# Soft mixture of experts, first 512 rows of x: from a casting load to float32 loads on two hardware queues with a cast on chip, and the first expert's products in two halves

## The chip, the cores and the metric

The kernel runs on one core of one Trainium2 chip. The metric is the device time of one execution in microseconds (us); lower is better. The profile is one execution taken by the hardware profiler; its times count from the start of its span. Engines: PE (TensorE, matmuls; PEld is its weight load), DVE (VectorE), ACT (ScalarE), POOL (GpSimd), SP (SyncE). A "q" behind an engine's name means its sequencer, which also issues transfers.

## The reference

```python
def setup_inputs():
    batch, seq, hidden, n_experts, expert_hidden = 16, 512, 512, 8, 2048
    ...

def reference(x, router_logits, expert_weights):
    probs = softmax(router_logits, axis=-1)
    ...
    for e in range(n_experts):
        expert_out = np.matmul(x, expert_weights[e])
        output += probs[:, :, e:e+1] * expert_out
    return output.astype(np.float32)
```

(The softmax is written out in the reference, with the maximum taken off first.) There are 8192 rows of x with 512 columns, 8 experts with weights of 512 x 2048 each, and an output of 8192 x 2048 float32. Every row's output is the sum over all experts of its probability times its product with that expert's weights.

## The kernel before, in words

**Arithmetic.** A row's sum over experts is one long product: x scaled by the probabilities of the experts, laid side by side, times the experts' weights stacked. The kernel cuts this product into quarters (rows in pairs of 256-row blocks, output columns in halves of 1024, experts in halves of four) and applies a seven-product scheme on two levels in place of eight products, with sums and differences of blocks made on DVE. So most of the program is: DVE makes a scaled left operand (`z`, float16), PE multiplies it with a block of weights (`w`, float16) into PSUM (`ps`), ACT or DVE evicts the result, and transfers carry it to HBM. These stages are laid out by a planner written by hand (`stages`, `at`, `slack`), which issues DVE's tasks by their costs; they begin at line 334 and the diff does not touch them.

**The opening, lines 80 to 332.** This is where the change lies. It computes a first product for 512 rows (row tiles `j` = 0 to 3 of 128 rows each, two from each of two 256-row blocks of x that lie 512 rows apart), four experts `e` and 1024 output columns (two blocks `n` of 512), without the two-level scheme, while the first weights are still on their way:

- Lines 80 to 89: ACT loads its table (L82), DVE clears a tile, and PE runs `WARM` = 10 matmuls on zeros (L89), which compute nothing that is used.
- `load_lg0(0)` (L206): the 512 rows' logits on SP's queue. `cast_x(0)`, `cast_x(2)` (L207, L208): two transfers on POOL's queue, of 256 rows of x each, float32 in HBM, cast by the transfer to float16 in `xs0`. [...]
- L213 to L219: the weights of the first block (`b11`), cast by POOL's queue too. `behind()` holds them behind what was issued so far. The first expert's load, for `n` = 0, is in two parts of two chunks (`c` = 0, 1 and 2, 3), the others are whole. Then two more x transfers (`cast_x(4)`, `cast_x(6)`) for later rows, and the last weights.
- `early_p(0)` (L244): the softmax of the 512 rows, on DVE with one ACT exponential (L179). `diag_e(e)` (L246): for expert e, DVE makes four diagonal matrices of its probabilities, 0.64 to 0.68 us each.
- `early_z0(e, d)` (L249): for each row tile j, four matmuls of 128 columns that transpose the four 128-column chunks of x and scale its rows at once (x's chunk times the diagonal matrix), into one PSUM bank; DVE (even j) or ACT (odd j) evicts the bank to `z0[j][:, e]` as float16.
- `load_logits()` (L279): SP loads the rest of the logits. Two memsets on DVE (L280, L281) keep these loads from being issued before DVE has come this far.
- The loop at L308: for `n` and `e`, 16 matmuls of 512 columns (4 chunks x 4 row tiles), chunk outermost, into four banks `ps[j]`. In the first round of `n`, `early_z0(e + 2)` stands ahead of the products of experts 0 and 1. So PE's order before is: transposes of experts 0, 1, 2; products of expert 0; transposes of expert 3; products of experts 1, 2, 3; then the second block.

**What sets the order.** Each engine runs its own list in order. `dve()`, `act()`, `sp()`, `pool()` and `mm()` record each instruction; those from `dve` and `act` stay in program order on their engine, so ACT's evictions and casts come in the order in which the code names them. Transfers of one queue are issued in order by their engine; a transfer that waits holds those behind it in the same list. PSUM has eight banks, given out by `bank()`.

Of the kernel before, what the change touches and what calls it, by code (L numbers as in the profile page):

```python
# [31 lines left out]
def kernel(  # L32
# [7 lines left out]
    nc = tc.nc  # L40
    P = 128
    f16 = mybir.dt.float16
    f32 = mybir.dt.float32
# [3 lines left out]
    B, S, H = x.shape  # L47
    E, _, EH = expert_weights.shape
    T = B * S
    C = H // P  # L50
    HE = E // 2
    NB = 512
    NH = EH // 2
    WARM = 10
    HQ = 256
    NHQ = T // HQ
    NI = NHQ // 2
# [2 lines left out]
    x_f = x.flatten_outer_dims()  # L60
# [3 lines left out]
    wpool = ctx.enter_context(tc.tile_pool(name="wpool", bufs=15))  # L64
# [9 lines left out]
    def h_tile(shape, dtype):  # L74
        return hpool.tile(shape, dtype, name="h", tag="h")

    def half():
        return h_tile([P, NB], f32)

    tiny = cpool.tile([P, 1], f32, name="tiny")  # L80
    nc.vector.memset(tiny, 0.0)
    nc.scalar.activation(out=tiny, in_=tiny, func=mybir.ActivationFunctionType.Exp)  # L82

    with tc.tile_pool(name="psum0", bufs=1, space=bass.MemoryType.PSUM) as psum0:
        zero = h_tile([P, NB], f16)
        nc.vector.memset(zero, 0.0)
        every = psum0.tile([P, 8, NB], f32, name="every")
        for i in range(WARM):
            nc.tensor.matmul(every[:, i % 8, :], zero[:, 0:P], zero, start=True, stop=True)  # L89
# [5 lines left out]
    def note(i):  # L95
        last[i.ins.engine] = i.ins
        if ordered[0]:
            tc.keep_in_program_order(i)

    def dve(i):  # L100
        last[i.ins.engine] = i.ins
        tc.keep_in_program_order(i)

    act = dve
# [12 lines left out]
    def sp(o, i):  # L117
        note(nc.sync.dma_start(out=o, in_=i))

    def pool(o, i, **how):  # L120
        note(nc.gpsimd.dma_start(out=o, in_=i, **how))  # L121

    def bank():
        return psum.tile([P, NB], f32, name="ps", tag="ps")

    def mm(ps, z, w, start, stop):
        note(nc.tensor.matmul(ps, z, w, start=start, stop=stop, skip_group_check=True))  # L127
# [3 lines left out]
    def new_w():  # L131
        return wpool.tile([P, K8, NB], f16, name="w", tag="w")
# [31 lines left out]
    def inner_sums(b, t7=None):  # L164

        w = {1: b[0, 0], 2: b[1, 0], 3: b[1, 1], 7: t7 or b[0, 1]}

        def step(p, x, y):
            if p not in w:
                w[p] = new_w()  # L170
            tt(w[p], x, y, SUB)
        return w, {5: lambda: step(5, b[0, 1], b[0, 0]), 6: lambda: step(6, b[1, 1], w[5]),
                   4: lambda: step(4, b[1, 0], w[6]), 7: lambda: step(7, b[1, 1], b[0, 1])}
# [15 lines left out]

    xs0 = new_w()  # L190

    ROWS = ("(p j) h -> p j h", "(j p) h -> p j h")

    def cast_x(j):
        pool(xs0[:, ds(j, 2), :], x_f[ds(j * HQ, HQ), :].rearrange(ROWS[j // 4], p=P))

    def load_lg0(t):
        rows = lg_f.rearrange("(q h) e -> q h e", h=2 * HQ)[ds(2 * t, 2), 0:HQ]
        tile_ = lg0[t].rearrange("p (q j) e -> p q j e", j=2)
        if t == 0:  # L200
            sp(tile_, rows.rearrange("q (p j) e -> p q j e", p=P))
        else:
            for q in range(2):
                sp(tile_[:, q], rows[q].rearrange("(j p) e -> p j e", p=P))
    lg0 = [cpool.tile([P, 4, E], f32, name=f"lg0_{t}") for t in range(2)]
    load_lg0(0)  # L206
    cast_x(0)  # L207
    cast_x(2)  # L208
    ident = cpool.tile([P, P], f16, name="ident")
    nc.vector.memset(ident, 1.0)  # L210
    nc.gpsimd.affine_select(out=ident, in_=ident, compare_op=mybir.AluOpType.is_equal, fill=0.0, base=0,
                            pattern=[[-1, P]], channel_multiplier=1)
    b11 = {kn: new_w() for kn in BLOCKS}  # L213
    with behind():
        for kn in BLOCKS[:3]:
            cast_block(11, kn, b11[kn], 2 if kn == (0, 0) else 1)
    cast_x(4)
    cast_x(6)
    cast_block(11, BLOCKS[3], b11[BLOCKS[3]])  # L219

    def early_p(t):
        if t == 0:
            return softmax(lg0[t], 4, cpool.tile([P, HE, 4], f16, name="ph0"))
        pf = softmax(lg0[t], 4, cpool.tile([P, HE, 4], f32, name="pf0"))
        odd = pf.rearrange("p e (q j) -> p e q j", j=2)[:, :, :, 1]
        tt(odd[:, 0:2], odd[:, 0:2], odd[:, 2:4], ADD)
        ph = cpool.tile([P, HE, 4], f16, name="ph1")
        dve(nc.vector.tensor_copy(ph, pf))
        return ph

    def diag(p):

        d = h_tile([P, 4, P], f16)
        tt(d, ident.unsqueeze(1).to_broadcast([P, 4, P]), p.to_broadcast([P, 4, P]), MUL)
        return d

    def evacuate(o, ps, i):
        if i % 2:
            act(nc.scalar.copy(o, ps))
        else:  # L240
            dve(nc.vector.tensor_copy(o, ps))  # L241

    z0 = [zpool.tile([P, HE, C, P], f16, name="z", tag="z") for j in range(4)]
    ph0 = [early_p(0)]  # L244

    def diag_e(e):  # L246
        return diag(ph0[0][:, e].unsqueeze(2))

    def early_z0(e, d):  # L249
        for j in range(4):  # L250
            ps = bank()
            for c in range(C):
                mm(ps[:, ds(c * P, P)], xs0[:, j, ds(c * P, P)], d[:, j], c == 0, c == C - 1)
            evacuate(z0[j][:, e], ps.rearrange("p (c t) -> p c t", c=C), j)
# [5 lines left out]
    def diag_j(j):  # L260
        return diag(ph0[1][:, :, ds(j % 4, 1)])

    def early_xp1(j, d):
        t, rows = j // 2 - 2, ds(j % 2 * P, P)
        ps = bank()
        for c in range(C):
            mm(ps[:, ds(c * P, P)], xs0[:, j, ds(c * P, P)], ident, c == 0, c == C - 1)
        evacuate(xp1[t][0][:, :, rows], ps.rearrange("p (c t) -> p c t", c=C), 0)
        ps = bank()
        mm(ps, ones, d.rearrange("p e t -> p (e t)"), True, True)  # L270
        evacuate(xp1[t][1][:, :, rows], ps.rearrange("p (e t) -> p e t", e=HE), 1)
# [7 lines left out]
    def load_logits():  # L279
        dve(nc.vector.memset(lg_all[:, 0, 0:1], 0.0))  # L280
        dve(nc.vector.memset(lg0[1][:, 0, 0:1], 0.0))  # L281
        load_lg0(1)
        for r in range(R):
            sp(lg_all[ds(r * NHQ, NHQ)], lg_v[r])

    def softmax_of_all():

        pf = softmax(lg_all, J, h_tile([P, E, J], f32))
        pq = h_tile([P, HE, J], f32)
        tt(pq, pf[:, 0:HE], pf[:, HE:E], ADD)  # L290
        low = ds(P // 2, P // 2)
        pv = pf.rearrange("p (s e) j -> p s e j", s=2)[low]
        tt(pv[:, :, 0:2], pv[:, :, 0:2], pv[:, :, 2:4], ADD)
        tt(pq[low, 0:2], pq[low, 0:2], pq[low, 2:4], ADD)
        ph = h_tile([P, 3 * HE, J], f16)
        act(nc.scalar.copy(ph[:, 0:E], pf))
        act(nc.scalar.copy(ph[:, E:], pq))
        for r in range(R):
            sp(p_dram[:, :, ds(r * J, J)], ph[ds(r * NHQ, NHQ)])

    kept = [dram.tile([2, HQ, NB], f32, name=f"kept_{i}") for i in range(NI)]

    ds_ = [diag_e(0), diag_e(1)]
    early_z0(0, ds_[0])
    ds_.append(diag_e(2))
    load_logits()
    early_z0(1, ds_[1])
    for n in range(2):  # L308
        ps = [bank() for _ in range(4)]
        for e in range(HE):  # L310
            if n == 0 and e < 2:
                early_z0(e + 2, ds_[e + 2])
                if e == 0:
                    ds_.append(diag_e(3))
            if n == 0 and e == 2:
                ph0.append(early_p(1))
                ds_ = [diag_j(j) for j in range(4, 8)]
                softmax_of_all()
                w, sums = inner_sums(b11, new_w())
            for c in range(C):  # L320
                for j in range(4):
                    mm(ps[j], z0[j][:, e, c], b11[e // 2, n][:, e % 2 * C + c, :],
                       e + c == 0, e == HE - 1 and c == C - 1)
            if n == 1:
                for j in ((4, 5), (6, 7), (), ())[e]:
                    early_xp1(j, ds_[j - 4])
                if e == 1:
                    sums[5]()
        for j in range(4):
            o = half()  # L330
            act(nc.scalar.copy(o, ps[j]))
            sp(kept[j // 2][n].rearrange("(p j) m -> j p m", j=2)[j % 2], o)
# [706 lines left out]
```

## Time and profile before

| | us |
|---|---|
| three runs, median (lowest to highest) | 1377.73 (1377.30 to 1377.74) |
| the profiled execution | 1377.86 |
| its span, first to last instruction | 1376.2 |
| PE busy | 1368.5 (99% of the span, 6390 matmuls) |
| DVE busy | 1108.8 (81%) |
| POOL busy | 412.3 (30%) |
| ACT busy | 183.3 (13%) |
| HBM read, written | 207.65 MB, 156.43 MB: 265 GB/s over the span |

The steady part of the kernel is matmuls of 512 columns, recorded with a mean of 379 ns each; they are pipelined, and start 0.216 us apart (16 in 3.46 us). A time "to landing" of a transfer counts from the start of its issue to the completion that others can wait for. Where a row of the timeline says `[0.80 <-DMA w<-in_x_dram]`, the engine was idle for 0.80 us before it, and the last thing that released it was that transfer. A row "x16" merges 16 instructions that follow each other, and its time runs from the first one's start to the last one's end; as matmuls overlap, the next row can start before that.

### The profile page before, as it was taken

The page shows a single profiled execution, that of the slowest core. Times are in us where ns is not written, and L with a number is a line of the kernel's source. Part 1 is how long each engine was busy: PE and PEld are TensorE (multiplying, and loading weights), DVE is VectorE, ACT ScalarE, POOL GpSimd, SP SyncE. Part 2 cuts the span into 40 slices and gives each one's busy share as a digit, 9 for nine tenths or more (in the row PEclk, how much of TensorE's full clock was granted, in tenths as well). Part 3 has the DMA queues.
Part 4 walks back from the last instruction along what each step waited for, and adds up shares of the span by engine and source line. Part 5 has one row for each costly group of instructions (what it writes and reads, how often), then busy time and mean ns, then how long its engine had stood idle before and what let it go on. Part 6 is the DMA issues. An engine that isn't in the chain of part 4 may idle for free.

```text
span 1376.2 us, 17481 instructions
## 1 busy us (share of the span) xinstructions
PE 1368.5 (99%) x6390; PEld 622.3 (45%) x6390; DVE 1108.8 (81%) x1290; ACT 183.3 (13%) x317; POOL 412.3 (30%) x652
## 2 busy tenths in 40 slices
PE   9999999999999999999999999999999999999998
PEld 4444444444444444444444444444444444444444
DVE  5846757679789888798887988889888898898782
ACT  3222111100011111111111100000000000222221
POOL 3222333231223342334332122333323322232321
PEclk9999999999999999999999999999999999999999
DMA  9997999999898998999897997988888979998785
GB/s 186 229 255 207 212 250 260 252 297 381 235 311 267 279 282 249 267 260 264 252 275 255 348 383 208 241 233 207 232 231 231 231 219 309 228 197 186 167 147 101
DMA packets 191271, 338.02 MB, mean 246 GB/s; under 512 B 52944, under 2 KB 86992, under 8 KB 187472
## 3 DMA queue, kind: packets, MB, share of 16 engines
q0 software_dynamic: 88688, 185.12, 55.8%
q1 hardware_dynamic: 98464, 123.34, 31.1%
q10 hardware_dynamic: 4032, 28.44, 5.3%
q8 instruction: 50, 0.82, 0.2%
q14 instruction: 37, 0.30, 0.1%
HBM read 207.65 MB, written 156.43 MB: 265 GB/s over the span
## 4 chain that ended last, share of the span: by engine, by line
PE 91%; issue 4%; DMA 3%; POOL 1%; DVE 1%; POOLq 0%; ACT 0%; DVEq 0%
PE ps L127 91%; POOL out_dram L121 1%; DMA out_dram<-h 1%; DMA w<-wd 1%; DMA w<-in_x_dram 0%; DVE h L107 0%; DVE z L107 0%; DVE u L107 0%; POOL wd L121 0%; DVE z L241 0%; POOL w L121 0%; ACT h L991 0%; POOLq L121 0%; DVEq L107 0%; DVE lg L281 0%
## 5 line engine op out<-in xcount | busy, mean ns | idle before, releaser
L127 PE MATMUL ps<-w,z 128*128 128x512 f16 x5416 | 1177.5, 379 | 2.1 <-DVE h L107 1.7
L127 PEld LDWEIGHTS <-z 128*128 128x128 f16 x5416 | 529.7, 98 | 639.8 <-issue 2.6
L121 POOL DMA_DIRECT2D out_dram<-h x380 | 249.2, 675 | 742.5 <-ACT h L536 369.1
L107 DVE TENSOR_TENSOR h<-ps,h 128x512 f32<-128x512 f32 x415 | 282.6, 688 | 207.8 <-PE ps L127 190.1
L107 DVE TENSOR_TENSOR z<-xT,pT 128x2048 f16<-128x2048 f16 x220 | 267.2, 1218 | 12.1 <-DMA xT<-xs 8.3
L127 PE MATMUL ps<-w,d 128*128 128x512 f16 x880 | 199.1, 379 | 0.0
L127 PEld LDWEIGHTS <-d 128*128 128x128 f16 x880 | 86.1, 98 | 103.8
L107 DVE TENSOR_TENSOR z<-z,d 128x2048 f16<-128x2048 f16 x110 | 132.2, 1217 | 0.0
L107 DVE TENSOR_TENSOR w<-w 128x1024 f16<-128x1024 f16 (+2 forms) x92 | 101.0, 1103 | 6.3 <-DMA wd<-w 3.9
L525 ACT COPY h<-ps 128x512 f32<-128x512 f32 x90 | 52.9, 587 | 375.0 <-PE ps L127 314.0
L536 ACT COPY h<-ps 128x512 f32<-128x512 f32 x64 | 37.6, 587 | 486.1 <-PE ps L127 459.7
L107 DVE TENSOR_TENSOR d<-z 128x1024 f16<-128x1024 f16 x110 | 75.4, 686 | 6.8 <-PE ps L127 5.0
L107 DVE TENSOR_TENSOR z<-z,u 128x2048 f16<-128x2048 f16 x64 | 78.4, 1225 | 2.2
L107 DVE TENSOR_TENSOR u<-xT,pT 128x2048 f16<-128x2048 f16 x64 | 78.0, 1219 | 0.0
L522 ACT COPY h<-ps 128x512 f32<-128x512 f32 x90 | 52.8, 587 | 173.8 <-PE ps L127 160.2
L121 POOL DMA_DIRECT2D wd<-w x86 | 48.4, 586 | 36.9 <-DVE w L107 27.4
L121 POOL DMA_DIRECT2D w<-in_expert_weights_dram x65 | 48.9, 783 | 34.2 <-DMA wd<-w 24.1
L107 DVE TENSOR_TENSOR ps<-ps,h 128x512 f32<-128x512 f32 (+1 forms) x66 | 45.4, 689 | 12.9 <-PE ps L127 12.9
L121 POOL DMA_DIRECT2D kept<-h x56 | 30.9, 551 | 75.5 <-ACT h L525 46.9
L107 DVE TENSOR_TENSOR h<-h 128x512 f32<-128x512 f32 (+2 forms) x69 | 45.1, 675 | 0.2
L518 ACT COPY ps<-ps 128x512 f32<-128x512 f32 x45 | 25.7, 572 | 114.6 <-PE ps L127 114.6
L107 DVE TENSOR_TENSOR z<-z 128x2048 f16<-128x2048 f16 x32 | 39.2, 1225 | 1.1
(47 smaller groups left out, 98.1 us busy)
## 6 DMA issues: line engine op xcount, KB each, us to landing
out_dram<-h POOLq DMA_DIRECT2D x380, 256.0 KB, 6.2
pT<-p_dram SPq DMA_DIRECT2D x140, 256.0 KB, 6.1
w<-wd ACTq DMA_DIRECT2D x27, 1024.0 KB, 9.8
h<-kept SPq DMA_DIRECT2D x100, 256.0 KB, 5.8
xT<-x SPq DMA_DIRECT2D x87, 256.0 KB, 5.8
wd<-w POOLq DMA_DIRECT2D x72, 256.0 KB, 5.8
w<-in_expert_weights_dram POOLq DMA_DIRECT2D x35, 512.0 KB, 10.1
h<-out_dram SPq DMA_DIRECT2D x68, 256.0 KB, 5.5
```

The costliest lines, as they stand in the source:

```text
L107: dve(nc.vector.tensor_tensor(out=o, in0=a, in1=b, op=op))
L121: note(nc.gpsimd.dma_start(out=o, in_=i, **how))
L127: note(nc.tensor.matmul(ps, z, w, start=start, stop=stop, skip_group_check=True))
L518: act(nc.scalar.copy(self.banks["b"], x))
L522: act(nc.scalar.copy(o[tn], q if p == 5 else x))
L525: act(nc.scalar.copy(o[TN[p]], b if p == 2 else x))
L536: act(nc.scalar.copy(o[tn], b))
```

## The change

1. The first 512 rows of x no longer come as float16 through POOL's casting queue. Two plain float32 transfers into a new tile `x32` take their place: rows of the first block on ACT's queue, as the first thing in the program, rows of the second on SP's queue behind the first logits. `x32` takes a buffer of the weight pool.
2. Four casts on chip fill `xs0`: tiles 0, 1 and 3 on ACT, tile 2 on DVE. ACT's list there becomes: cast tile 0, cast tile 1, evict tile 1, cast tile 3, further evictions. DVE's: diagonals of expert 0, evict tile 0, cast tile 2, evict tile 2, diagonals of experts 1 and 2, the two memsets, further evictions.
3. The products of expert 0 for the first block come in two halves of the rows: all chunks for tiles 0 and 1, then the transposes of expert 1, all chunks for tiles 2 and 3, then the transposes of expert 2. The transposes of expert 3 follow the products of expert 1. All other products stay as they were.
4. `WARM` is 9 and not 10.

```diff
-    WARM = 10
+    WARM = 9
...
+    x32 = wpool.tile([P, 4, H], f32, name="x32", tag="w")
+    x_first = [x_f[ds(2 * q * HQ, HQ), :].rearrange("(p j) h -> p j h", p=P) for q in range(2)]
+    nc.scalar.dma_start(out=x32[:, 0:2, :], in_=x_first[0])
     tiny = cpool.tile([P, 1], f32, name="tiny")
...
     load_lg0(0)
-    cast_x(0)
-    cast_x(2)
+    sp(x32[:, 2:4, :], x_first[1])
...
-    def early_z0(e, d):
-        for j in range(4):
+    def early_z0(e, d, js=range(4)):
+        for j in js:
...
-    ds_ = [diag_e(0), diag_e(1)]
-    early_z0(0, ds_[0])
-    ds_.append(diag_e(2))
+    ORDERS = ([(c, j) for c in range(C) for j in range(4)],
+              [(c, j) for h in range(2) for c in range(C) for j in (2 * h, 2 * h + 1)])
+    ds_ = [diag_e(0)]
+    for j in range(2):
+        act(nc.scalar.copy(xs0[:, j, :], x32[:, j, :]))
+    early_z0(0, ds_[0], (0, 1))
+    dve(nc.vector.tensor_copy(xs0[:, 2, :], x32[:, 2, :]))
+    act(nc.scalar.copy(xs0[:, 3, :], x32[:, 3, :]))
+    early_z0(0, ds_[0], (2, 3))
+    ds_ += [diag_e(1), diag_e(2)]
     load_logits()
-    early_z0(1, ds_[1])
     for n in range(2):
         ps = [bank() for _ in range(4)]
         for e in range(HE):
-            if n == 0 and e < 2:
-                early_z0(e + 2, ds_[e + 2])
-                if e == 0:
-                    ds_.append(diag_e(3))
+            if n == 0 and e == 1:
+                ds_.append(diag_e(3))
...
-            for c in range(C):
-                for j in range(4):
-                    mm(ps[j], z0[j][:, e, c], b11[e // 2, n][:, e % 2 * C + c, :],
-                       e + c == 0, e == HE - 1 and c == C - 1)
+            for c, j in ORDERS[n == 0 and e == 0]:
+                mm(ps[j], z0[j][:, e, c], b11[e // 2, n][:, e % 2 * C + c, :],
+                   e + c == 0, e == HE - 1 and c == C - 1)
+                if n == 0 and c == C - 1 and (e, j) in ((0, 1), (0, 3), (1, 3)):
+                    early_z0(1 + e + j // 3, ds_[1 + e + j // 3])
```

In the lists of instructions that the two programs give each engine, this is all that differs; behind the opening, every engine's list is the same in both.

More of the change, by code (lines that the diff above doesn't have):

```diff
@@ L190 @@
     xs0 = new_w()
-    ROWS = ("(p j) h -> p j h", "(j p) h -> p j h")
     def cast_x(j):
-        pool(xs0[:, ds(j, 2), :], x_f[ds(j * HQ, HQ), :].rearrange(ROWS[j // 4], p=P))
+        pool(xs0[:, ds(j, 2), :], x_f[ds(j * HQ, HQ), :].rearrange("(j p) h -> p j h", p=P))
     def load_lg0(t):
```

## The prediction

> **What bounds the kernel now.** I read the busy table first: PE is busy 1368.5 of 1376.2 us. Then the chain of waits, to see whether anything ahead of the steady matmul stream sets the end. Its first 40 us:
>
> ```profile
> 1.33 0.67 POOL w L121
> 2.00 4.86 DMA w<-in_x_dram
> 6.91 0.41 PE ps L127 x4
> 7.35 0.69 DVE z L241
> 8.04 0.60 DVE h L107
> 8.64 0.05 DVE lg L281
> 8.69 31.51 PE ps L127 x180
> ```
>
> The reader is to see that the end hangs on the x load (cast by the DMA, issued by POOL) until 6.9 us, on VectorE until 8.7, and from there on TensorE alone (in the chain over the whole span that piece of PE runs on from 8.69 for 776.79 us). So the opening can matter only through the moment at which TensorE begins to run without a gap. The waits by engine say the same: PE waits in five places, 4.0 us in all over the span.
>
> The opening in the timeline, engine by engine (start, length, engine, line, operation, count):
>
> ```profile
> 1.29 4.45 PE L89 MATMUL every<-h 128*128 128x512 f16 x10 [1.29 <-DVE h L86]
> 5.64 0.77 PEld L127 LDWEIGHTS <-w 128*128 128x128 f16 x8 [0.80 <-DMA w<-in_x_dram]
> 6.40 0.69 DVE L241 CAST z<-ps 128x512 f16<-128x512 f32 x1 [0.94 <-PE ps L127]
> 6.62 0.59 ACT L239 CAST z<-ps 128x512 f16<-128x512 f32 x1 [3.21 <-PE ps L127]
> 9.76 3.63 PE L127 MATMUL ps<-w,z 128*128 128x512 f16 x16
> 13.22 1.06 PE L127 MATMUL ps<-h,w 128*128 128x128 f16 x16
> 14.11 13.98 PE L127 MATMUL ps<-w,z 128*128 128x512 f16 x64
> 24.82 0.62 ACT L296 CAST h<-h 128x512 f16<-128x512 f32 x1 [3.37 <-DVE h L107]
> ```
>
> One expert's scaled transposes (early_z0, 16 matmuls of 128 columns) hold TensorE from 13.22 to 14.11, 0.89 us; one expert's products (16 of 512 columns) from 9.76 to 13.22, 3.46 us. Issue to landing of single transfers (KB written, last figure in us), the first x half issued at 1.33, the first two chunks of the first expert at 2.90, the logits at 0.81:
>
> ```profile
> w<-in_x_dram POOLq DMA_DIRECT2D x1, 256.0 KB, 4.3
> w<-in_expert_weights_dram POOLq DMA_DIRECT2D x1, 256.0 KB, 6.8
> lg<-in_router_logits_dram SPq DMA_DIRECT2D x1, 16.0 KB, 1.9
> ```
>
> So x's first half landed at 5.6, its second at 6.86 (the end of the DMA piece in the chain), and the first weights at 9.7: TensorE's weight load of 9.75 had waited 0.17 us for them.
>
> **The break-even.** The order of instructions of the two programs differs in the opening alone; afterwards every engine's list is the same. Before, products begin at 9.76 with three experts' transposes done. After, they begin with one done; two blocks of 0.89 follow among the products. If TensorE then runs without a gap, the change breaks even where the first product starts at 9.76 - 2 x 0.89 = 7.98 us. Call the new start P; the effect is P - 7.98.
>
> **The change, part by part.**
> *Removed from POOL:* two issues (0.67 and about 0.6 us, with first x at 1.33 and first weights at 2.90), so weights are issued 1.57 us sooner. *Added:* one x half each on ACT's and SP's queues. An issue costs ACT about 0.4 us (SP's logit issues take 0.42 to 0.46, and ACT's last store 0.37), which moves the table load of 0.81 to 1.28 us later; its exp of the logits at 3.18 has 0.88 us of idle time before it, so this is hidden, and would cost up to 0.4 if that cover went. On SP the x half goes behind the first logits and ahead of all other loads; the only one issued right behind it is half of the second logits, needed at 15.19. *One warm-up matmul less:* ten take 4.45 us, so the nine end about 0.43 sooner, at 5.1 for what follows them. Worth something only if x is ready then.
>
> *Landing of x's first half (L).* No row shows 512 KB in float32 on an idle hardware queue. Low end: 0.81 + 1.9 (logit row) + 1.27 (what the second half took after the first, 6.87 - 5.60, which is 512 KB read) = 4.0; the logits' own data is in the 1.9, so 3.8 is thinkable. High end: 0.81 + 4.3 (this very load, other queue) + 1.27 for the other half interleaved with it = 6.4. I take 4.6, the hardware row plus half of the second half's 1.27: its fixed part is from the nearest row in kind of queue, and the two queues share the engines. By the load's own row without sharing it would be 5.1.
>
> [...]
>
> *The new serial chain behind L.* ACT's list is now: cast row tile 0, cast tile 1, evict tile 1's transposes, cast tile 3. So: 0.05 to react (landing 5.60, weight load 5.64); two casts at 0.62 (the ACT cast of 128x512 float32 from SBUF, row L296), 1.24; tile 1's four matmuls until they can be evicted 0.76 (5.64 to 6.40 for four) plus 0.04; eviction 0.59; third cast 0.62; 0.04; four matmuls and on to the product, 0.16 for the load and 4 x 0.056 (0.89 / 16), 0.4. Sum 3.74, P = L + 3.7. VectorE's branch is shorter: tile 0's eviction 0.69 and tile 2's cast (no row; between 0.35, half of the nearest, and 0.69 of an eviction from PSUM) end before ACT's third cast. Break-even: L = 4.3. With 4.6, P = 8.3 and the effect is **+0.3 us**.
> *Floor.* However early x comes, TensorE is on its warm-up until 5.1; eight matmuls to eviction 0.82 (6.62 - 5.80), then 0.59 + 0.62 + 0.04 + 0.4: P at least 7.6. The gain cannot pass 0.4 us.
>
> *Weights.* The first chunks: at best 1.33 + 6.8 - 2 x 1.27 = 5.6 (both x loads gone from ahead), at worst 1.33 + 6.8 = 8.1 (the same bytes still ahead, through interleaving). Both lie before 8.3, so I cost this wait at nothing; behind an early x it would be next. The next chunks (needed at P + 0.87 = 9.2) come 1.3 later, 6.9 to 9.4. The expert's second load had 13.7 as its landing and is needed at P + 2 x 1.73 + 2 x 0.89 = 13.5, now issued 1.57 sooner.
> *Moved on VectorE:* two diagonals (2 x 0.65) and the two marker memsets that release the logit loads (8.59 before) now stand behind tile 2's eviction, about 1 us later. The logits feed reductions at 15.19 that end in diagonals by 19.5, which TensorE first reads at 28.15, and probabilities stored at 25.8 whose reloads SP issues only at 42.05, behind stores. That cover is 8 us and more; nothing.
> Casts and evictions add about 2.5 us of ACT and VectorE work there; both idle in that stretch.
>
> **Sum.** Span 1376.2 + 0.3; the profiled execution took 1377.86, of which 1.66 lie around the span, and stands 0.13 over the median of 1377.73. On the median: 1378.0 us.
>
> **Rivals.**
> 1. *x is early after all* (L of 3.8 to 4.0). For it: the logits' 1.9 us. Against it: they are 16 KB, and x on POOL's queue took 4.3. P = 7.6 to 7.7, effect -0.3 to -0.4: 1377.4.
> 2. *The loads interleave, the first expert's weights with them* (L of 5.5 to 6.4). For it: DMA's share is 0.8 to 1.4 in every half microsecond from 4.0 us on. P = 9.2 to 10.1, +1.2 to +2.1: about 1379.2. The logits could also be held behind x's packets: they would delay the first diagonal, which must then end 1.0 us later (4.8 now, 5.8) before it costs anything.
> 3. *TensorE stays slow* (slower than before). The records of its matmuls change in the opening: 128-column matmuls have a mean of 284 ns in 5.7 to 6.2 us and 220 from 6.9 on, and the warm-up's ten of 512 columns have 631 against 379 later; the step falls near 6.2, 4.9 us after the first of them, though the granted clock shows 1.00 all along. Ten warm-ups in 4.45 us are 0.43 apart, products 0.216: half the pace. After the change TensorE idles from 5.1 until 5.4, again between tiles 0 and 1, and for over a microsecond ahead of tile 2, where before there were gaps of 0.06, 0.33 and 0.27. If that makes it stay slow past P, every us of it costs 0.5. From 4.9 us of it (as long as the first stretch) with the 0.3 it is +2.75, 1380.5: from there it decides. One us or two, and it is 1379.
> [...]
> 4. *That it doesn't do what it says* is excluded by the lists of instructions: ACT's first entry is the x load.
>
> **How the numbers follow.** Forecast (between -0.2 and +0.9) 0.44; rival 1 0.18; rival 2 0.20; rival 3 0.18, about half of it at 4.9 us or more. The range of 1377.2 to 1379.7 reaches over rival 1 and most of rival 2, and leaves out the long form of rival 3 and the end of rival 2; the forecast's own is 1377.5 to 1378.6. 0.2% of 1377.7 is 2.76 us, about what a measurement of this kernel can tell from no change. Faster by that is beyond the floor of 0.4 us: 0.02, for what I overlooked. Slower by that needs the long form of rival 3, or rivals 2 and 3 together: 0.10. Within it: 0.88.
>
> **What would show it.** In the new timeline: x's first half casts on ACT at 4.65 (L); the products of 512 columns first at 8.3 (P) and no gap behind them; ACT's third cast ending 0.4 before P; weight loads waiting for no weights; the first products 0.216 apart, else rival 3; the first diagonal still ending at 4.8. Wrong altogether would be a gap of TensorE later than 20 us that was not there, or a span that moves by another amount than P - 7.98.

## The result, and the profile after

| | median, us | runs | lowest to highest |
|---|---|---|---|
| before | 1377.74 | 6 | 1377.30 to 1378.42 |
| changed | 1382.47 | 6 | 1381.36 to 1384.00 |

The ratio is 1.0035 with a 95% interval of 1.0022 to 1.0048: slower by 4.7 us, 3.0 to 6.6 by the interval. The profiled execution of the changed kernel took 1382.42 us, its span 1380.7 (1376.2 before). The prediction had 1378.0.

The opening after the change, from the timeline of TensorE (start, length, engine, line, operation, count):

```profile
1.29 4.02 PE L92 MATMUL every<-h 128*128 128x512 f16 x9 [1.29 <-DVE h L89]
7.05 1.01 PE L130 MATMUL ps<-h,w 128*128 128x128 f16 x8 [1.73 <-DVE h L110]
8.75 1.11 PE L130 MATMUL ps<-h,w 128*128 128x128 f16 x8 [0.69 <-DVE w L309]
9.66 3.62 PE L130 MATMUL ps<-w,z 128*128 128x512 f16 x8
13.07 1.35 PE L130 MATMUL ps<-h,w 128*128 128x128 f16 x16
14.26 1.89 PE L130 MATMUL ps<-w,z 128*128 128x512 f16 x8
```

Three things are in these rows. The first transposes begin at 7.05, after a wait of 1.73 us for VectorE's diagonal (h, L110), not for x. The first product begins at 9.66, against a break-even of 7.98. And the first eight products hold TensorE from 9.66 to 13.07, 3.41 us, where the second eight (14.26 to 15.99) need 1.73: the first eight run at half pace. The records of the granted clock in this trace begin with full pace at 13.68.

Why the diagonal is late stands in the chain of waits:

```profile
0.81 3.94 DMA lg<-in_router_logits_dram
4.78 0.20 DVE h L180
5.23 0.24 ACT lg L182
6.21 0.70 DVE h L110
7.05 0.60 PE ps L130 x4
```

The chain now begins with the logits, 16 KB that landed 1.9 us after issue before the change and 3.9 after it. They hold up x as well: its first half had landed at 4.57, but ACT's list has the exponential of the logits ahead of the two casts.

```profile
5.23 0.23 ACT L182 ACTIVATE lg<-lg 128x32 f32<-128x32 f32 x1 [2.46 <-DVE lg L110]
5.36 1.12 ACT L307 CAST w<-x 128x512 f16<-128x512 f32 x2
```

The transfers issued in the first microsecond (KB, then us to landing) show what is beside the logits:

```profile
x<-in_x_dram ACTq DMA_DIRECT2D x1, 512.0 KB, 3.8
lg<-in_router_logits_dram SPq DMA_DIRECT2D x1, 16.0 KB, 3.9
```

Both were issued at 0.81, on two queues, and the small one landed after the large one. In the packet records of the trace, x's half runs first (128 packets from 1.9 us on), 255 of the logits' 256 packets start only after 3.0, and the second x half (SP's queue) and the weights (POOL's) follow nearly one after the other, most of the one from 4.0 on and all of the other from 5.1 on.

A second loss lies at 31 us. VectorE, ACT and TensorE in the timeline after the change, and behind them the same reduction and the same evictions before it:

```profile
21.96 0.17 DVE L180 TENSOR_REDUCE h<-lg 128x4 f32<-128x32 f32 x1
27.57 0.63 ACT L182 ACTIVATE h<-h 128x512 f32<-128x512 f32 x1 [4.93 <-DVE h L110]
31.57 0.62 ACT L296 CAST h<-h 128x512 f16<-128x512 f32 x1 [3.37 <-DVE h L110]
32.40 2.04 ACT L336 COPY h<-ps 128x512 f32<-128x512 f32 x4
33.12 0.38 PE L130 MATMUL ps<-ident,w 128*128 128x128 f16 x4 [1.37 <-ACT h L336]
```

```profile
15.19 0.19 DVE L177 TENSOR_REDUCE h<-lg 128x4 f32<-128x32 f32 x1 [0.26 <-DMA lg<-in_router_logits_dram]
25.65 2.04 ACT L331 COPY h<-ps 128x512 f32<-128x512 f32 x4
```

The first reduction of the remaining logits starts at 21.96 (15.19 before), though the load that it needs was issued at 11.72 and had landed at 17.5 (5.8 us). VectorE's list has the evictions of expert 3's transposes ahead of it, and those transposes moved behind expert 1's products (20.34 and not 13.22). ACT's list has its evictions of the first block's banks (L336) behind the exponential and casts of that softmax, so they start at 32.40 (25.65 before), and TensorE, which needs a bank for the next transposes, stands idle.

From the starts of the same matmuls in both traces, the changed kernel is 3.66 us behind from 18 to 28 us, 5.26 behind from 34 on, and 4.27 at the last one: later waits of TensorE for VectorE have shrunk, most of it near 1180 us. These late waits differ from execution to execution: from 34 us to the end, the lag changes by -1.4 to +0.6 us in the traces of the runs below. The first figure splits: 1.68 of late first product (9.66 - 7.98), 1.68 of half pace in eight products (3.41 - 1.73), 0.29 in the transposes behind them (13.07 to 14.26 is 1.19, such a block is 0.89).

### The profile page after: what moved, and what is told of

Its sections match the earlier page's. It is cut to its first block, busy times and chain, and to the rows that moved or that the text cites. A ratio compares the mean times of both kernels' runs of the same rounds, so it can differ in the third digit from the quotient of the medians.

```text
span 1380.7 us, 17484 instructions
## 1 busy us (share of the span) xinstructions
PE 1370.4 (99%) x6389; PEld 623.2 (45%) x6389; DVE 1109.3 (80%) x1291; ACT 184.6 (13%) x320; POOL 411.1 (30%) x650
## 4 chain that ended last, share of the span: by engine, by line
PE 77%; issue 12%; DMA 6%; POOL 4%; DVE 1%; ACT 0%; SPq 0%; POOLq 0%; ACTq 0%; DVEq 0%
PE ps L130 77%; POOL out_dram L124 3%; DMA out_dram<-h 2%; DMA wd<-w 1%; DMA w<-wd 1%; POOL wd L124 1%; DVE h L110 1%; DMA xs<-in_x_dram 1%; DMA h<-kept 0%; DMA lg<-in_router_logits_dram 0%; POOL w L124 0%; SPq L402 0%; DVE z L110 0%; DVE u L110 0%; DVE z L241 0%
## 5 line engine op out<-in xcount | busy, mean ns | idle before, releaser
L110 DVE TENSOR_TENSOR h<-ps,h 128x512 f32<-128x512 f32 x415 | 282.4, 688 | 208.3 <-PE ps L130 188.3
L110 DVE TENSOR_TENSOR z<-xT,pT 128x2048 f16<-128x2048 f16 x220 | 267.1, 1218 | 12.0 <-DMA xT<-xs 6.9
L110 DVE TENSOR_TENSOR z<-z,d 128x2048 f16<-128x2048 f16 x110 | 132.2, 1217 | 0.0
L110 DVE TENSOR_TENSOR w<-w 128x1024 f16<-128x1024 f16 (+2 forms) x92 | 101.0, 1103 | 5.2 <-DMA wd<-w 2.9
L110 DVE TENSOR_TENSOR d<-z 128x1024 f16<-128x1024 f16 x110 | 75.4, 686 | 6.8 <-PE ps L130 5.0
L110 DVE TENSOR_TENSOR z<-z,u 128x2048 f16<-128x2048 f16 x64 | 78.4, 1225 | 2.2
L110 DVE TENSOR_TENSOR u<-xT,pT 128x2048 f16<-128x2048 f16 x64 | 78.0, 1218 | 0.0
L110 DVE TENSOR_TENSOR ps<-ps,h 128x512 f32<-128x512 f32 (+1 forms) x66 | 45.4, 689 | 12.6 <-PE ps L130 12.5
L110 DVE TENSOR_TENSOR h<-h 128x512 f32<-128x512 f32 (+2 forms) x69 | 45.1, 675 | 0.4 <-ACT h L530 0.3
L110 DVE TENSOR_TENSOR z<-z 128x2048 f16<-128x2048 f16 x32 | 39.2, 1225 | 1.1
```

The lines of the kernel that those rows point to most:

```text
L110: dve(nc.vector.tensor_tensor(out=o, in0=a, in1=b, op=op))
```

## The experiments

Each row is against the kernel before on the same chip (its median in brackets). The last column is read from the one traced execution of each run: how far the matmuls that the kernel before starts at 34 us start behind it.

| run | median, us | against before | 95% interval of the ratio | behind at 34 us, trace |
|---|---|---|---|---|
| changed kernel | 1382.47 (1377.74) | +4.7 | 1.0022 to 1.0048 | 5.3 |
| 16 warm-ups | 1380.09 (1377.57) | +2.5 | 1.0009 to 1.0028 | 3.1 |
| logits first, one queue | 1381.05 (1377.57) | +3.5 | 1.0019 to 1.0043 | 6.5 |
| expert 3's transposes back | 1381.17 (1377.57) | +3.6 | 1.0016 to 1.0035 | 3.1 |
| logits first, two queues | 1381.19 (1377.59) | +3.6 | 1.0017 to 1.0036 | 3.4 |
| warm-ups and transposes back | 1378.67 (1377.36) | +1.3 | 1.0002 to 1.0019 | 1.7 |
| all three repairs | 1378.79 (1377.59) | +1.2 | 0.9997 to 1.0016 | 1.4 |
| repairs and another order | 1377.71 (1377.36) | +0.4 | 0.9993 to 1.0012 | -0.1 |
| before, 6 warm-ups | 1378.14 (1377.57) | +0.6 | 0.9996 to 1.0015 | 0.4 |
| before with float32 loads alone | 1381.64 (1377.59) | +4.1 | 1.0018 to 1.0043 | 3.6 |
| before with two halves alone | 1382.17 (1377.59) | +4.6 | 1.0020 to 1.0041 | 4.9 |

The intervals of the single repairs overlap that of the changed kernel, so what one repair gives is read from its trace as well as from its median; the two repairs together lie clear of it.

My theory after the result: the loss has three causes, late logits, half pace after an idle start, and the moved transposes of expert 3. The rivals: x's landing or the weights set the start; the pace comes back by itself; the late logits loads make the wait at 31.

**1. More warm-ups in the changed kernel** (`e1_warm16`).

```diff
-    WARM = 9
+    WARM = 16
```

> The changed kernel with 16 warm-up matmuls in place of 9, nothing else. In the changed kernel TensorE idles from 5.1 to 7.05 us and its matmuls stay at the slow pace (0.427 us apart for 512 columns) until 13.7. Theory (the idle keeps TensorE slow, worth about 2.0 us: 8 products at 0.427 and not 0.216, and transposes at 0.107 and not 0.056): warm-ups cover the idle, the products of expert 0 come 0.216 apart, the first transposes still wait for the diagonal until about 7, and the time falls by 2.0 to 2.5 us, to about 1380.2. Rival (the late start alone costs the time, the pace would recover by itself): no change, 1382.5; or later still, if 16 slow warm-ups end at 8.1.

Measured: 1380.09, +2.5 against the kernel before where the changed kernel has +4.7: 2.2 less. From its timeline of TensorE:

```profile
1.30 6.05 PE L92 MATMUL every<-h 128*128 128x512 f16 x16 [1.30 <-DVE h L89]
7.40 0.61 PE L130 MATMUL ps<-h,w 128*128 128x128 f16 x8
9.44 1.89 PE L130 MATMUL ps<-w,z 128*128 128x512 f16 x8
11.16 1.06 PE L130 MATMUL ps<-h,w 128*128 128x128 f16 x16
```

The first product starts 0.2 us earlier only; the first eight now take 1.72 us (9.44 to 11.16) in place of 3.41. Matmuls that compute nothing used, added to the start, made the program faster. The clock records of this trace have full pace from 6.23 on (13.68 in the changed kernel). The theory's part on the pace holds.

**2. The pace in the kernel before** (`b1_warm6`).

```diff
-    WARM = 10
+    WARM = 6
```

> The kernel before with 6 warm-up matmuls in place of 10, so that TensorE idles from 3.9 to 5.8 us; nothing else is touched, and nothing waits for a warm-up. Theory (an idle of two us at the start keeps TensorE at the slow pace): the transposes and the first products run at half pace, until 9.6 or 13; 1.0 to 2.5 us slower, 1378.7 to 1380.2. Rival (the pace changes at 6.2 whatever TensorE did before): 1377.7.

Measured: 1378.14, and the interval holds 1; I had expected 1.0 to 2.5. In its trace the matmuls do stay slow longer: 128-column starts are 0.107 us apart until 8.9 (until 6.2 with ten warm-ups), then 0.056, so the rival (the pace changes at 6.2 whatever TensorE did) falls.

```profile
7.07 3.28 PE L127 MATMUL ps<-h,w 128*128 128x128 f16 x40 [0.61 <-DMA w<-in_x_dram]
10.18 3.62 PE L127 MATMUL ps<-w,z 128*128 128x512 f16 x16
```

But in the kernel before only transposes stand there, and the products behind them wait for weights anyway: the first product starts at 10.18 and not 9.76. In this execution the weights landed at 10.0 and not 9.7, so the pace itself cost only about 0.1 of these 0.4 us. What stands behind the gap sets what the half pace costs: about 0.1 us here, on transposes, and 1.68 in the changed kernel, on eight products.

**3. Expert 3's transposes back in their place** (`e3_z3_back`).

```diff
             if n == 0 and e == 1:
                 ds_.append(diag_e(3))
+                early_z0(3, ds_[3])
...
-                if n == 0 and c == C - 1 and (e, j) in ((0, 1), (0, 3), (1, 3)):
+                if n == 0 and c == C - 1 and (e, j) in ((0, 1), (0, 3)):
```

> The changed kernel with the transposes of expert 3 ahead of the products of expert 1 again, as before. Theory (with them behind, VectorE's list holds the softmax of the remaining logits behind expert 3's evictions, 7 us later; ACT's evictions of the first block stand behind that softmax's exponential, and TensorE waits 1.5 us for a bank at 31.4): the softmax's first reduction at about 17.5 and not 21.96, no gap of TensorE near 31, and the time falls by 1.4 to 1.6 us, to 1381. Rival (the gap follows from the late logits loads, which the memsets at 11.25 released late): the gap stays, 1382.5.

Measured: 1381.17, +3.6 and so 1.1 less than the changed kernel (1.4 to 1.6 expected), and the wait at 31 is gone, though the reduction moved only to 19.14 and not to the 17.5 expected:

```profile
19.14 0.17 DVE L180 TENSOR_REDUCE h<-lg 128x4 f32<-128x32 f32 x1
29.58 2.04 ACT L337 COPY h<-ps 128x512 f32<-128x512 f32 x4
30.92 0.39 PE L130 MATMUL ps<-ident,w 128*128 128x128 f16 x4
```

The last row has no bracket: TensorE did not wait. The lists of VectorE and ACT are the same as in the changed kernel; only the place of sixteen matmuls on TensorE differs. The logits that the reduction needs land as late as in the changed kernel (at 17.55 in both), so the rival falls. In the trace this run is 2.2 us less behind than the changed kernel; 1.5 of it is the wait, and the rest stands at the start, where the first product came at 9.16 though nothing ahead of it differs (the last section comes back to this).

**4. Logits ahead of x on one queue** (`e2_logits_first`): both x halves on SP behind the logits.

```diff
-    nc.scalar.dma_start(out=x32[:, 0:2, :], in_=x_first[0])
...
+    sp(x32[:, 0:2, :], x_first[0])
     sp(x32[:, 2:4, :], x_first[1])
```

> The changed kernel with both x halves on SP's queue behind the first logits, none on ACT's. Theory (the logits' packets stood behind x's first half on the 16 engines, 2 us late, and so the softmax and the first diagonal): logits land at about 2.8 and not 4.76, the first diagonal ends at 4.9 and not 6.9, x's first half lands at about 5.1 (issued 0.5 later than on ACT), the first transposes run at about 5.8 and the first product at 8.5 and not 9.66: 1.1 us less by that alone, and up to 2 more if the shorter idle lets TensorE come to its full pace sooner: 1379.5 to 1381.4. Rival (x's landing and the two casts in series set the start, not the logits): no gain or 0.5 us later, 1382.5 to 1383.

Measured: 1381.05 in the median, from 1379.96 to 1385.14; the profiled execution is the slowest of them. The logits landed at 2.55, the diagonal ended at 4.7, x's first half landed at 5.05 and the first transposes ran at 5.75, all as the theory had it. Then a new wait, which neither side had foreseen:

```profile
5.75 0.92 PE L129 MATMUL ps<-h,w 128*128 128x128 f16 x8 [0.43 <-ACT w L307]
9.54 1.04 PE L129 MATMUL ps<-h,w 128*128 128x128 f16 x8 [2.88 <-DVE w L309]
10.37 3.62 PE L129 MATMUL ps<-w,z 128*128 128x512 f16 x8
```

The second x half, third in SP's queue, landed at 9.0; packets of the weights ran beside it from 3.9 us on, where in the changed kernel they started at 5.15. Why two loads in one queue give way to the weights and two in two queues do not, no run here shows. TensorE idled again, and the products ran at half pace (10.37 to 13.78).

**5. Logits ahead of x on two queues** (`e5_x0_later`): a memset of one column of x32 on VectorE, which ACT's load has to wait for, moves its issue from 0.81 to 1.26. (The clearing of the warm-ups' zero tile moves ahead of it.)

```diff
+    zero = h_tile([P, NB], f16)
+    nc.vector.memset(zero, 0.0)
+    nc.vector.memset(x32[:, 0, 0:1], 0.0)
     nc.scalar.dma_start(out=x32[:, 0:2, :], in_=x_first[0])
```

> The changed kernel with one small memset on VectorE into x32 ahead of ACT's x load, so that this load is issued at about 1.2 and not 0.81, behind the logits' issue; both hardware queues are kept. Theory (the 16 engines serve the logits' packets behind those of whichever large load was there first): the logits land at about 2.6 and not 4.76, the first diagonal ends at 4.8, x's halves land at about 5.1 and 5.9 (in the run with both halves on SP's queue the second came at 9.0, behind weights), first product at about 8.6, 1.0 earlier; with the pace recovering earlier up to 2 more: 1379.5 to 1381.4. Rival (a hardware queue of ACT holds up SP's small load whatever comes first): logits at 4.5 or later, 1382.5.

Measured: 1381.19, +3.6 and so 1.1 less than the changed kernel.

```profile
lg<-in_router_logits_dram SPq DMA_DIRECT2D x1, 16.0 KB, 1.9
6.10 0.92 PE L131 MATMUL ps<-h,w 128*128 128x128 f16 x8 [1.34 <-ACT w L308]
8.62 3.03 PE L131 MATMUL ps<-w,z 128*128 128x512 f16 x8
```

The logits landed at 2.74, the diagonal ended at 4.9, x's halves at 5.4 and 6.2, the first product started at 8.62. So an issue 0.45 us later on another engine brought 16 KB in 2 us sooner; the rival (ACT's queue holds up SP's whatever comes first) falls. By the trace's clock records the pace, full from 4.1 on, was half from 7.5 to 10.9, behind an idle of 1.34 us at 4.8 and shorter ones.

**6. One part of the change alone** (`b2_float_only`, `b3_halves_only`). The first has the float32 loads and casts with the old order and 10 warm-ups; the second the new order with POOL's casting loads and 10 warm-ups. Against the kernel before, the core of the second is:

```diff
-            for c in range(C):
-                for j in range(4):
-                    mm(ps[j], ...)
+            for c, j in ORDERS[n == 0 and e == 0]:
+                mm(ps[j], ...)
+                if n == 0 and c == C - 1 and (e, j) in ((0, 1), (0, 3), (1, 3)):
+                    early_z0(1 + e + j // 3, ds_[1 + e + j // 3])
```

> The float32 loads on two hardware queues and the casts on chip alone: order of transposes and products and 10 warm-ups as in the kernel before. Theory: diagonal at 6.9 as in the changed kernel, expert 0's transposes until 9.6, then those of experts 1 and 2 before the first product, at 11.5 to 12 (9.76 before), with most of the slow pace on transposes and the end of it on products: 1.8 to 3 slower, 1379.6 to 1380.7; no gap near 31, as expert 3's transposes are in their old place. Rival (the loads cost nothing, the two halves do): 1377.6.

> The two halves and the moved transposes alone: x cast by POOL's queue and 10 warm-ups as in the kernel before. Theory: the weights land at 9.7 as before, so TensorE idles from 7.4 to 9.75 with expert 0's transposes done, where before it made those of experts 1 and 2: 1.8 slower by that, and the late softmax of the remaining logits (expert 3's evictions ahead of it) brings the wait near 31, 1.5: 1380.5 to 1381.2, more if the idle slows the pace. Rival (halves cost nothing): 1377.6.

Measured: 1381.64 and 1382.17. Each part alone is slower by about as much as both together (4.1 and 4.6 against 4.7), so they don't add. The loads alone:

```profile
7.09 0.61 PE L130 MATMUL ps<-h,w 128*128 128x128 f16 x8 [1.35 <-DVE h L110]
10.37 3.19 PE L130 MATMUL ps<-h,w 128*128 128x128 f16 x32 [1.08 <-DVE h L110]
13.40 3.62 PE L130 MATMUL ps<-w,z 128*128 128x512 f16 x16
```

The late diagonal is there; a second wait for a diagonal (expert 1's stands behind tile 2's eviction) and 32 slow transposes put the first product at 13.40, 3.64 after the 9.76 of before, more than the 12 I had expected. The halves alone, from the timeline and then from the view of stretches (us, busy time of PE, PEld, DVE, ACT, POOL with counts, granted clock, DMA share, GB/s):

```profile
9.75 3.41 PE L127 MATMUL ps<-w,z 128*128 128x512 f16 x8 [1.84 <-DMA w<-in_expert_weights_dram]
32.75 0.38 PE L127 MATMUL ps<-ident,w 128*128 128x128 f16 x4 [1.37 <-ACT h L331]
```

```profile
6.00:9.00 3.00, 1.13 (x16) 0.84 (x15) 1.96 (x4) 1.17 (x2) 2.82 (x4) 1.00 0.85 128
9.00:12.00 3.00, 2.25 (x6) 0.86 (x6) 0.64 (x4) 0.00 (x0) 1.48 (x2) 0.58 1.23 201
12.00:13.00 1.00, 1.00 (x5) 0.30 (x3) 0.00 (x0) 0.00 (x0) 0.00 (x0) 0.56 1.24 206
13.00:15.00 2.00, 2.00 (x23) 1.41 (x22) 1.29 (x2) 1.07 (x2) 0.74 (x1) 1.00 1.33 219
```

Weights that land at 9.7 as before leave TensorE idle for want of the transposes that used to fill the time; after a stretch with 1.13 us of work in 3.00 the granted clock is 0.58, and the products run at half pace. The wait for a bank is in this run too (1.37 us at 32.75), as expected, and not in the run with the loads alone. So the halves need earlier weights, which the loads on other queues do bring (the first part landed at 8.1 in the changed kernel). Late first products and half pace stand in both runs; that is why the two losses don't add, as far as these traces tell.

**7. Do the causes add up?** (`e8_warm_z3`, `e6_all`): 16 warm-ups with edit 3; and edits 3 and 5 with 12 warm-ups.

> The changed kernel with 16 warm-ups and expert 3's transposes ahead of expert 1's products again; the logits stay late. Theory (three causes that add up, 2.4 for the pace and 1.3 to 1.6 for the softmax): the first product stays at 9.4, 1.4 to 1.5 behind 7.98, no gap near 31: 1378.8 to 1379.1. Rival (the causes overlap, one repair takes what the other gave): 1380 or more.

> All three repairs in one: x's first half issued behind the logits' issue, 12 warm-up matmuls, expert 3's transposes ahead of expert 1's products again. Theory (late logits, slow pace and late softmax make up the loss, and what is left is the new start of the first product against 7.98): first product at 8.3 to 8.8, paces of 0.216 from it on, no gap near 31: 0.3 to 0.9 over the kernel before, 1378.0 to 1378.6. Rival (some of the loss lies elsewhere, in the float32 traffic or the weights): 1379.5 or more.

Measured: +1.3 and +1.2, 1378.67 (a little under the forecast) and 1378.79 (a little over it). Two repairs take 4.7 to 1.3, about what the pace (2.2) and the softmax (1.1) had given one by one; within the noise they add. In the first of the two runs the logits are late and the pace is full:

```profile
7.11 0.61 PE L130 MATMUL ps<-h,w 128*128 128x128 f16 x8 [0.81 <-DVE h L110]
9.14 1.89 PE L130 MATMUL ps<-w,z 128*128 128x512 f16 x8
```

The logits' repair (with 12 warm-ups in place of 16) gives nothing more that can be seen: the two intervals overlap, and the runs of one median spread over 2 us. So what the late logits cost is shown for the start of the products (8.57 below, 9.14 above) and not for the whole time. The timeline of the second run shows what takes their place:

```profile
6.15 0.92 PE L131 MATMUL ps<-h,w 128*128 128x128 f16 x8 [0.69 <-ACT w L308]
7.66 0.40 PE L131 MATMUL ps<-h,w 128*128 128x128 f16 x4 [0.60 <-DVE w L310]
8.57 1.02 PE L131 MATMUL ps<-w,z 128*128 128x512 f16 x4
9.83 1.02 PE L131 MATMUL ps<-w,z 128*128 128x512 f16 x4 [0.24 <-DMA w<-in_expert_weights_dram]
```

TensorE now waits for the casts, then starts products at 8.57, 0.6 after the break-even, and stands again for the second part of the weights, which landed at 9.8: in halves, TensorE wants it 0.87 us after its first product.

**8. Another order on top of the repairs** (`e7_order`): casts spread over ACT and VectorE ahead of the evictions, transposes of experts 0 and 1, expert 0's products chunk by chunk over all rows, then the transposes of experts 2 and 3. Against the run with all three repairs, in part:

```diff
+    ds_ = [diag_e(0), diag_e(1)]
+    for j in range(4):
+        if j % 2:
+            dve(nc.vector.tensor_copy(xs0[:, j, :], x32[:, j, :]))
+        else:
+            act(nc.scalar.copy(xs0[:, j, :], x32[:, j, :]))
+    early_z0(0, ds_[0])
...
+    early_z0(1, ds_[1])
...
+                early_z0(2, ds_[2])
                 early_z0(3, ds_[3])
...
-            for c, j in ORDERS[n == 0 and e == 0]:
+            for c, j in ORDERS[0]:
...
-                if n == 0 and c == C - 1 and (e, j) in ((0, 1), (0, 3)):
-                    early_z0(1 + e + j // 3, ds_[1 + e + j // 3])
```

> The run with all three repairs, with another order: casts spread over ACT (tiles 0 and 2) and VectorE (1 and 3) and ahead of all evictions; transposes of experts 0 and 1, then expert 0's products as before (not in halves), then the transposes of experts 2 and 3. Its break-even is 9.76 less one block of transposes, 8.87. Theory (what is left in the repaired run, +1.2, is the chain of casts and evictions behind x's landing and then the weights): first transposes at about 6.0, first product at the weights' landing, 8.4 to 8.6, so 0.3 to 0.5 under the kernel before: 1377.2. Rival (float32 loads cost elsewhere): 1378.6 or more.

Measured: 1377.71 against 1377.36, interval 0.9993 to 1.0012: no difference from the kernel before, where 0.3 to 0.5 less was expected.

```profile
8.54 3.61 PE L131 MATMUL ps<-w,z 128*128 128x512 f16 x16
```

In its trace the first product starts at 8.54 and TensorE is 0.13 us ahead of the kernel before from 16 us on. No version here beats it measurably. A cost of the float32 loads elsewhere, or of the buffer that `x32` takes, is not to be seen within this interval (-1.0 to +1.7 us).

## Why the prediction was wrong, point by point

**Step "The new serial chain behind L", "P = 8.3": mis-sized by 1.36 us.** The number of L was right (4.6 predicted, 4.57 measured), in part by luck: half of 1.27 us was added for the other half of x, on the ground that the two queues share the engines. No run shows that term: in the trace of the changed kernel 127 of the first half's 128 packets had started by 4.0 us, and only 7 of the second half's 128. The weights' landing (5.6 to 8.1 predicted, 8.1 measured) and VectorE's cast (0.35 to 0.69, measured 0.42) were right. The chain was hung on x alone. The logits were costed at nothing in the forecast; a sentence in rival 2 named the way in which they could be late, and even the point from which it costs (a diagonal at 5.8), but gave it no time. The diagonal ended at 6.9, and the logits came 2.0 us later than before; the 1.27 us that I had used for 512 KB of x would have been a first price for them, and still too low. Three first products split the 1.36: 9.66 in the changed kernel, 9.14 with late logits at full pace, 8.57 with logits in time at full pace (and x's first half landing 0.9 later, at 5.45). So, by these single traces, about 0.5 is half pace in the transposes and about 0.6 the logits. The chain itself was sized too long, which hid a part: 3.1 us in that last run against 3.7.

**Rival 3's mechanism gave the largest part, and the forecast costed it at nothing and left it at 18%.** The idle of TensorE that the change makes was listed, the slow pace of the first matmuls was read from the rows, and the price of 0.5 us a microsecond was right: from 9.66 to 13.7 the pace was half, 1.68 on the products and 0.29 on transposes, and 16 warm-ups took 2.2 away. What was missing is that the pace would last so long: the forecast had none of it behind P, rival 3 gave it one to five microseconds, and it was 4.0. The prediction priced "one warm-up matmul less" as time saved, if x was ready; with the first transposes at 7.05, it only made the gap longer.

**Step "Moved on VectorE ... That cover is 8 us and more; nothing" failed.** It followed the two diagonals and the memsets, about 1 us, and not the evictions of expert 3, which moved by 7 us in time (13.64 to 20.76) without moving in VectorE's list. The cover was also taken to the wrong reader: not the matmul at 28.15 that reads the diagonals, but ACT, whose evictions of the first block stand behind the softmax in its list, and the matmul that needs their bank. 1.6 us in the trace, 1.1 in the median of the runs with the transposes back.

**The floor** (the gain cannot pass 0.4 us) stood: the best repaired order is level with the kernel before. The span moved by other than P - 7.98, which the prediction named as what would show it wrong altogether.

The span's 4.5 us are, by these two traces: 1.7 late start, 2.0 pace, 1.6 wait for a bank, less 1.0 that later waits absorbed, and 0.3 behind the last matmul. No run tests the last two. So the late logits of rival 2 and the slow pace of rival 3 came together, which the prediction put into its 0.10 above the range, and the wait for a bank, which it had at nothing, came on top.

## What to carry to other kernels

- A step moved on one engine moves in time whatever other engines list behind its results. Follow those lists to the first wait of the engine that sets the end; an unchanged order is no sign of an unchanged time (experiment 3: sixteen matmuls moved on TensorE, and with the same list ACT's evictions began at 29.58 and not 32.40).
- Before a large load is issued first, look for a small one that a serial chain hangs on: here 16 KB on SP's queue landed 3.9 us after issue with 512 KB issued on ACT's queue at the same moment, and 1.9 us after issue with that load issued 0.45 us later.
- The gap of TensorE in the opening had two prices here, a first product 1.68 us late and the half pace behind it, 2.0 us. What stands behind the gap decides the second: with transposes there, and products that wait for weights anyway, it was about 0.1 us (experiment 2).

## What the runs showed of the hardware that I had not expected

- Whole loads passed nearly one after the other in the changed kernel though they stood in three queues: x's first half (128 packets, from 1.9 us), the logits (most from 3.5), the second half (from 4.0), the weights (from 5.1). In experiment 4 the second half ran beside the weights from 3.9 us on. What decides between the two, no run here shows.
- In the halves run the trace's clock records have the full pace granted at 6.05, half at 9.46 and full again at 12.88: steps of 3.41 us. The rows on the half pace stand in experiment 6. The half pace was granted within the second of two gaps of TensorE, 0.79 us ahead of 7.29 and 1.84 ahead of 9.75, each shorter than one such step.
- Where these steps fall differs between executions. The changed kernel and the run with expert 3's transposes back have the same lists up to there, but the first transposes took 1.01 us (half pace until 13.68) in the one trace and 0.61 in the other (full pace from 5.61, half from 9.03 to 12.44). Both lost 1.6 to 1.7 us on the first eight products (3.35 and 3.41 in place of 1.73).
- In the changed kernel the granted clock of the stretch from 9 to 12 us reads 1.00, ahead of the first clock record at 13.68, while matmuls of 512 columns took 631 ns there against 379 later. The duration of a known matmul is the safer reading of the pace.
